# A hybrid decoder layer: the opening in finer slices, and other priorities for the second half

## The chip, the core and the metric

The kernel runs on one core of a Trainium2 chip. Its time is device microseconds of one execution. The engines are TensorE (PE, with weight loads as PEld), VectorE (DVE), ScalarE (ACT), GpSimd (POOL) and SyncE (SP), which here issues nearly all DMAs. A change of about 1% of this kernel's time can be told from none.

## The reference

One layer works on x, 1024 rows (positions) of 1024 columns, all in float32. `mod` below is a product of a conditioning vector with w_ada (1024 x 6144), cut into six rows of 1024: shift, scale and gate of the two sub-layers.

```
h    = rmsnorm(x, g_mix) * (1 + sc1) + sh1
proj = h @ w_in                      # q 512, k 128, v 128, qi 512, ki 64, wi 8, cu 1024 columns
q, k, qi, ki = rope on the first quarter of each 64-wide head
score[t, s] = sum over 8 heads of wi[t] * relu(qi[t] . ki[s] / 8),  only s <= t
sel  = the 256 best s of each t      # causal top-k
attn = softmax(q . k[sel] / 8) @ v[sel]              # 8 heads, 2 key heads
conv = silu(layernorm(depthwise causal conv, width 31, of glu(cu)))   # 512 channels
x    = x + gt1 * (concat(attn, conv) @ w_out)
h    = rmsnorm(x, g_mlp) * (1 + sc2) + sh2
x    = x + gt2 * (square(relu(h @ w_up)) @ w_down)                    # width 4096
out  = rmsnorm(x, g_final)
```

## The kernel before

The 1024 rows are 8 blocks of 128, in two halves: blocks 0 to 3 and 4 to 7. Columns of 1024 are 8 pieces k of 128. Nearly every product is made of three: both operands are split into a rounded high part and the low part that is left, and high x high, high x low and low x high are summed in PSUM. So for every weight piece ScalarE writes the high part and GpSimd the low part (`load_unit`, L161 to L186; `load_w`, L147).

The code is written in the Tile framework, which orders each engine's instructions by itself: each instruction has a priority number (`tc.cur_priority`, from the table `PR` in L54; a lower number goes first among those that a model of the chip holds ready), and instructions of one engine then run in that fixed order. Buffers are handed out in the order of the code: a tile with `bufs=2` waits for the tile two before it, whatever the priorities. The weight units share one ring: two raw buffers and three of high and low parts, each cut into halves (L163 to L175).

**The opening** (`start` pool, L239 to L420) makes h, transposed and split (`hT`), and the products with the 328 columns of w_in for k, v, ki and wi.
- `START` (L49) is the order of SyncE's loads: x0 to x7 are the blocks of x, a0 to a3 the slices of w_ada for shift and scale (each four loads of 512 KB into two of the four `wa` buffers), p0 to p2 the three pieces of k/v weights.
- `row_scale` (L283) takes four blocks' mean squares (even blocks by ScalarE, L290, odd ones by VectorE, L287), their inverse roots, and a diagonal matrix `dg` for each block (L296). `transposes` (L305) multiplies x by `dg`, which transposes and scales it at once, and ScalarE copies the result to `xT`.
- `ada` (L312) is VectorE's running sum over the eight pieces of a slice of w_ada, in SBUF; `ada_end` (L321) has TensorE add up the 128 partitions and puts shift and scale for two pieces k into `modT`.
- `h_cols` (L331) scales and shifts one piece k of one half on VectorE (L334), takes the high part on ScalarE (L335) and the low part (L336) on VectorE for the first half's pieces below `LOV` = 6, on GpSimd for the others.
- `kv` (L340) makes the products of four blocks with one piece k.
- `WORK` (L50) is the order of these steps. Behind them stand the second half's `h_cols`, the angles and their sine and cosine (L373 to L412).

**After the opening** come the second half's k/v products (priority `k`), the keys for attention and indexer, and three more parts of w_ada, 24 loads of 512 KB with VectorE's sums behind them (`ada_part`, L512; the load is L517, the sum L521, TensorE's part of it L537). The rest follows `ORDER` (L46) and `TAIL` (L44): Q and q are the projections of indexer queries and queries (0 for the first half, 1 for the second; they go out to DRAM, L563, and come back by block, L567), g the gate units of the convolution, c the convolution of the first half (31 taps on VectorE, L643), i the index scores of a block, s a search of the 256th best score of two blocks by 31 halvings (ScalarE counts, L680; VectorE steps, L682 and L683), S the selection from it (L686 to L711), a the attention of a block, n and z the convolution's norm and output, o the output projection, h the norm ahead of the MLP. The first half's MLP (11 of its 16 groups of columns, `f11`) has nearly the lowest priority and fills TensorE while the second half's search, selection and attention run. What is left of the MLP runs at the end, from about 904 us.

Of the kernel before, what the change touches and what calls it, by code (L numbers as in the profile page):

```python
# [9 lines left out]
FT = mybir.dt.float32  # L10
# [3 lines left out]
U8 = mybir.dt.uint8  # L14
AF = mybir.ActivationFunctionType
# [37 lines left out]
LOV = 6  # L53
PR = {'feed': 32050, 'evac': 30050, 'k': 150500, 'qi': 33500, 'ada': 130000, 'idx': 200000, 'idx2': 207550, 'small': 149500, 'sign': 150050, 'sign0': 205450, 'select': 401450, 'select0': 207500, 'att0': 205500, 'norm0': 190500, 'out0': 207000, 'res0': 30000, 'conv0': 998450, 'conv1': 401000, 'q': 400000, 'qi1': 401000, 'q1': 401500, 'glu': 206500, 'glu1': 410000, 'att1': 33450, 'norm1': 998500, 'out1': 150000, 'res1': 206000, 'upx': 215900, 'vhl': 411500, 'hd0': 213500, 'hd7': 399950, 'sq3': 997950, 'mlp': 1000000}  # L54
# [18 lines left out]
def layer(ctx, tc, x, c, positions, w_ada, b_ada, g_mix, w_in, conv_w, conv_b,  # L73
# [165 lines left out]
    with tc.tile_pool(name="start", bufs=1, reuse_waits="tile") as st:  # L239
# [37 lines left out]

        xT = st.tile([128, KD, S], FT, name="xT")
        ms, rs, tmp1 = (st.tile([128, 8], FT, name=n) for n in ("ms", "rs", "tmp1"))
        junk = st.tile([128, D], U8, name="junk")  # L280
        dg = {}

        def row_scale(g0):  # L283
            for b in range(g0, g0 + 4):
# [6 lines left out]
            col = slice(g0, g0 + 4)  # L291
            V.tensor_scalar(ms[:, col], ms[:, col], 1.0 / D, EPS, op0=OP.mult, op1=OP.add)
            rsqrt(rs[:, col], ms[:, col], tmp1[:, col], 4)
            for b in range(g0, g0 + 4):
                dg[b] = st.tile([128, 128], FT, name="dg", bufs=4)
                V.tensor_scalar(dg[b], ident, rs[:, b:b + 1], None, op0=OP.mult)  # L296

        for hf in range(2):  # L300
            hT[hf] = (half_tile("AC"[hf]), half_tile("BD"[hf]))
        pa = psum.tile([128, 16], FT, name="po")

        def transposes(b):
            for q in range(2):  # L305
                t = tp_tile()
                for j in range(4):
                    k = 4 * q + j
                    T.matmul(t[:, j, :], xs[b][:, k * 128:(k + 1) * 128], dg[b], start=True, stop=True)  # L309
                A.copy(xT[:, 4 * q:4 * q + 4, b * 128:(b + 1) * 128], t)  # L310

        def ada(jj):  # L312
            acc = st.tile([128, 512], FT, name="acc", bufs=2)
            for k in range(KD):
                if k:
                    V.scalar_tensor_tensor(acc, was[jj, k // 4 * 4][:, k % 4, :], cond[:, k:k + 1], acc, op0=OP.mult, op1=OP.add)  # L316
                else:
                    V.tensor_scalar(acc, was[jj, k // 4 * 4][:, k % 4, :], cond[:, 0:1], None, op0=OP.mult)
            return acc

        def ada_end(jj, acc):  # L321
            for i in range(4):
                c0 = 8 * (i // 2) + 2 * jj + i % 2
                T.matmul(pa[:, c0:c0 + 1], acc[:, i * 128:(i + 1) * 128], ones[:, 0:1], start=True, stop=True)
            s0, s1 = slice(2 * jj, 2 * jj + 2), slice(8 + 2 * jj, 10 + 2 * jj)
            V.tensor_tensor(modT[:, s0], pa[:, s0], bada[:, s0], op=OP.add)
            a1 = modT[:, s1]
            V.tensor_tensor(a1, pa[:, s1], bada[:, s1], op=OP.add)
            V.scalar_tensor_tensor(a1, a1, 1.0, gmix[:, s0], op0=OP.add, op1=OP.mult)

        def h_cols(k, hf):  # L331
            hi, lo = hT[hf]
            xk = xT[:, k, hf * 512:(hf + 1) * 512]
# [4 lines left out]
        kvps = {}  # L338

        def kv(k, blocks):  # L340
            for i, b in enumerate(blocks):
                if k == 0:
                    kvps[b] = (mm_tile if i < 2 else mc_tile)(328)
                hi, lo = hblk(b, k, 0), hblk(b, k, 1)
                wh, wl = pieces[k]
                for j, (l, r) in enumerate(((hi, wh), (lo, wh), (hi, wl))):
                    T.matmul(kvps[b], l, r, start=k == 0 and j == 0, stop=k == KD - 1 and j == 2)

        row_scale(0)
        accs = {}  # L350
        for step in WORK.split():
            n = int(step[1:])
            if step[0] == "a":
                accs[n] = ada(n)
            elif step[0] == "t":
                transposes(n)
            elif step[0] == "r":
                row_scale(n)
            elif step[0] == "e":
                ada_end(n, accs[n])  # L360
            elif step[0] == "h":
                for k in (2 * n, 2 * n + 1):
                    h_cols(k, 0)
            elif step[0] == "k":
                for k in (2 * n, 2 * n + 1):
                    kv(k, KVG[0])
            elif step[0] == "g":
                for k in (2 * n, 2 * n + 1):
                    h_cols(k, 1)
        for k in range(KD):  # L370
            if k // 2 not in [int(x[1:]) for x in WORK.split() if x[0] == "g"]:
                h_cols(k, 1)
# [36 lines left out]
        A.activation(sn, rr, AF.Sin)  # L409
        A.activation(ml, rr, AF.Abs)  # L410
        V.tensor_scalar(ml, ml, -1.0, 1.5707963267948966, op0=OP.mult, op1=OP.add)
        A.activation(cs, ml, AF.Sin)  # L412
# [852 lines left out]
```

## Time and profile before

| | us |
|---|---|
| median of 3 runs | 1372.71 (1371.03 to 1380.61) |
| profiled execution | 1377.54 |
| its span | 1375.8 |
| TensorE busy (matmuls) | 1268.3, 92% |
| VectorE busy | 974.8, 71% |
| ScalarE busy | 683.5, 50% |
| GpSimd busy | 482.0, 35% |
| DMA | 139.55 MB, mean 101 GB/s |
| mean granted TensorE clock | 0.964 |

Times in a trace are microseconds from the start of the span, durations of single instructions nanoseconds where marked. An engine's busy share is an average over stages with different limits; what counts is which wait ends last in a stage. A matmul counts as busy from its start to a modelled end, and matmuls overlap, so their number in a stretch says more than their busy time. The granted clock is the share of TensorE's full speed that it was allowed; its two levels are 1.2 and 2.4 GHz.

### The profile page before, as it was taken

The numbers are of one execution on the slowest core, as the hardware profiler recorded it, in microseconds if no ns is written. First come the engines' busy times: TensorE is split into PE (matmuls) and PEld (weight loads), VectorE is DVE, ScalarE is ACT, GpSimd is POOL, SyncE is SP. The second block draws the span as 40 slices with busy tenths as digits, with TensorE's granted clock in tenths as the row PEclk, the third lists the DMA queues.
The fourth block names the chain that finished last, engine by engine and source line by source line (L and its number), as shares of the span: only waits on it lengthen the run. The fifth ranks groups of instructions, "written<-read, shape, count | busy, mean of one in ns | idle before, by whom it ended". The sixth has DMA issues, their size and how long they took to land.

```text
span 1375.8 us, 19421 instructions
## 1 busy us (share of the span) xinstructions
PE 1268.3 (92%) x6686; PEld 1065.7 (77%) x6686; DVE 974.8 (71%) x2074; ACT 683.5 (50%) x1376; POOL 482.0 (35%) x396
## 2 busy tenths in 40 slices
PE   4677899989998899989999999899999999999997
PEld 4676789978887678767887879777878877888875
DVE  4879889999898899997878762473443386343457
ACT  3323358855764888768983552333122223333332
POOL 1333434422144234452223216422222244444453
PEclk9688999999999899999999999999999999999999
DMA  9337735522143123222111122352111134323332
GB/s 319 121 115 224 226 79 155 139 62 70 31 139 110 60 70 93 92 70 61 62 47 54 62 77 85 130 192 83 47 45 49 54 107 162 93 91 101 94 98 91
DMA packets 135690, 139.55 MB, mean 101 GB/s; under 512 B 8877, under 2 KB 109833, under 8 KB 135592
## 3 DMA queue, kind: packets, MB, share of 16 engines
q1 hardware_dynamic: 135424, 138.22, 32.2%
q8 instruction: 52, 0.85, 0.3%
q14 instruction: 46, 0.38, 0.1%
q10 hardware_dynamic: 168, 0.11, 0.0%
HBM read 126.23 MB, written 12.06 MB: 101 GB/s over the span
## 4 chain that ended last, share of the span: by engine, by line
PE 68%; DVE 21%; DMA 4%; issue 3%; ACT 3%; POOL 1%; ACTq 0%; POOLq 0%; DVEq 0%; SPq 0%
PE mm L126 25%; PE mc L126 13%; PE mm L137 9%; PE tp L126 7%; DMA wa<-in_w_ada_dram 3%; PE po L841 2%; PE tp L834 2%; DVE acc L521 2%; DVE cv L643 1%; PE tp L309 1%; PE po L748 1%; PE mc L592 1%; DVE acc L1018 1%; PE mc L822 1%; DVE acc L316 1%
## 5 line engine op out<-in xcount | busy, mean ns | idle before, releaser
L185 POOL TENSOR_TENSOR wlo<-wraw,whi 128x512 fp32r<-128x512 f32 x310 | 416.7, 1352 | 754.2 <-ACT whi L184 698.0
L184 ACT ACTIVATE whi<-wraw 128x512 fp32r<-128x512 f32 x310 | 193.9, 629 | 292.1 <-PE mm L126 143.1
L126 PE MATMUL mm<-half,whi 128*128 128x512 f32 x608 | 207.4, 407 | 0.6 <-ACT half L957 0.6
L680 ACT ACTIVATE sj<-score,bits 128x512 uint8<-128x512 f32 (+5 forms) x186 | 163.2, 877 | 23.0 <-DVE bits L683 11.0
L643 DVE SCALAR_TENSOR_TENSOR cv<-glu,cwT,cv 128x512 f32<-128x512 f32 x232 | 174.0, 750 | 0.8
L126 PE MATMUL mm<-whi,uh 128*128 128x512 f32 x344 | 141.7, 412 | 14.3 <-DVE sq L979 8.2
L126 PE MATMUL mc<-half,whi 128*128 128x512 f32 x416 | 149.0, 390 | 0.1
L126 PE MATMUL mm<-whi,ul 128*128 128x512 f32 x344 | 138.8, 404 | 3.0 <-DVE ul L986 3.0
L126 PE MATMUL mm<-wlo,uh 128*128 128x512 f32 x344 | 139.4, 405 | 0.0
L984 DVE TENSOR_TENSOR sq<-sq 128x512 f32<-128x512 f32 x42 | 46.0, 1096 | 126.1 <-ACT sq L983 126.1
L1018 DVE TENSOR_TENSOR acc<-mm,acc 128x512 f32<-128x512 f32 x152 | 104.3, 687 | 39.8 <-PE mm L126 38.9
L126 PE MATMUL mc<-half,wlo 128*128 128x512 f32 x336 | 131.1, 390 | 0.0
L126 PEld LDWEIGHTS mm<-half,whi 128*128 128x128 f32 x608 | 114.2, 192 | 20.0 <-ACT half L957 0.8
L137 PE MATMUL mm<-whi,half 128*128 128x256 f32 x640 | 121.8, 286 | 3.2 <-DVE wi L450 3.0
L126 PE MATMUL mm<-half,wlo 128*128 128x512 f32 x304 | 123.1, 405 | 0.0
L137 PEld LDWEIGHTS mm<-whi,half 128*128 128x128 f32 x640 | 102.9, 194 | 5.7 <-issue 3.1
L126 PE MATMUL mc<-h,whi 128*128 128x512 f32 x256 | 99.9, 390 | 0.0
L126 PEld LDWEIGHTS mm<-whi,uh 128*128 128x128 f32 x344 | 66.5, 193 | 37.0 <-DVE sq L979 10.8
L137 PE MATMUL mm<-wlo,half 128*128 128x256 f32 x320 | 91.2, 285 | 0.0
L126 PEld LDWEIGHTS mc<-half,whi 128*128 128x128 f32 x416 | 78.0, 188 | 16.6 <-ACT half L957 0.5
L126 PEld LDWEIGHTS mm<-whi,ul 128*128 128x128 f32 x344 | 66.6, 194 | 18.7 <-DVE ul L986 4.3
L126 PEld LDWEIGHTS mm<-wlo,uh 128*128 128x128 f32 x344 | 66.8, 194 | 13.2
(312 smaller groups left out, 2657.4 us busy)
## 6 DMA issues: line engine op xcount, KB each, us to landing
wraw<-in_w_up_dram SPq DMA_DIRECT2D x108, 256.0 KB, 2.8
wraw<-in_w_down_dram SPq DMA_DIRECT2D x108, 256.0 KB, 2.8
wa<-in_w_ada_dram SPq DMA_DIRECT2D x48, 512.0 KB, 4.5
wraw<-in_w_in_dram SPq DMA_DIRECT2D x33, 256.0 KB, 2.8
wraw<-in_w_in_dram SPq DMA_DIRECT2D x64, 128.0 KB, 2.9
wraw<-in_w_out_dram SPq DMA_DIRECT2D x32, 256.0 KB, 2.7
xs<-in_x_dram SPq DMA_DIRECT2D x8, 512.0 KB, 4.5
x<-in_x_dram SPq DMA_DIRECT2D x8, 512.0 KB, 4.3
```

Of the source, the lines that this page charges most:

```text
L126: T.matmul(ps, x, y, start=first and i == 0, stop=last and i == 3 * n - 1)
L137: T.matmul(ps[:, i * 256:(i + 1) * 256], rows[i][k][x], w[k][y], start=m == 0, stop=m == len(steps) - 1)
L184: A.activation(hi, raw, AF.Copy)
L185: P.tensor_tensor(lo, raw, hi.bitcast(FT), op=OP.subtract)
L309: T.matmul(t[:, j, :], xs[b][:, k * 128:(k + 1) * 128], dg[b], start=True, stop=True)
L521: V.scalar_tensor_tensor(accs[s], w, cond[:, k:k + 1], accs[s], op0=OP.mult, op1=OP.add)
L643: V.scalar_tensor_tensor(y if tap == CK - 1 else s, gl[:, tap:tap + 512], cwT[:, j, tap:tap + 1], s, op0=OP.mult, op1=OP.add)
L680: A.activation(sj[:, :L], score[b], AF.Sign, bias=bits[:, col].bitcast(FT), accum_out=cnt[:, col])
L834: T.transpose(t[:, 2 * i + u, :], sbp[u][:, (i0 + i) * 128:(i0 + i + 1) * 128], ident)
L841: T.matmul(po[:, hp % 2], vhl[:, i0 + i, g].rearrange("p a d -> p (a d)"), p[:, 2 * i:2 * i + 2, :], start=i0 + i + j == 0, stop=i0 + i == ...
L984: V.tensor_tensor(sq, sq, sq, op=OP.mult)
L1018: V.tensor_tensor(acc[b][:, cols], ps, acc[b][:, cols], op=OP.add)
```

## The change

In the opening:
- ScalarE takes all squares, and scales x itself by the inverse root (`row_scale`), so that the transposes are plain ones; `dg` is gone.
- The angles are computed ahead of everything else; only sine and cosine are left as a step of their own (T).
- `ada` is cut into three steps (pieces 0 and 1, 2 to 4, 5 to 7), and its running sum lies in PSUM.
- `h_cols` becomes `h_hi` and `h_lo`. ScalarE makes the high part straight from the transposed x, VectorE makes the whole value and the low part, for all pieces and both halves. The second half's x is transposed piece by piece and read from PSUM, so `xT` holds one half.
- `START` loads p0 right after x0, a1 ahead of four blocks of x, and p1 ahead of the rest of x.

In the order of the rest: q1 stands ahead of S3 in `ORDER`. In `PR`, the selection of blocks 4 to 7 goes from 401450 to 52550, the second half's convolution norm from 998500 to 129950, the first half's q projection from 400000 to 412000, the first half's search from 205450 to 207050, its gate units from 206500 to 205500, the second half's output projection from 150000 to 206450, and the MLP from 1000000 to 998000.

```diff
-ORDER = "Q0 g0 i2 c q0 i3 s3 Q1 m S3 q1 a0 g1 a1 n0 a2 z0 a3 i6 i7 o i5 h i4 s7 s5"
+ORDER = "Q0 g0 i2 c q0 i3 s3 Q1 m q1 S3 a0 g1 a1 n0 a2 z0 a3 i6 i7 o i5 h i4 s7 s5"
-START = "x0 x1 x2 x3 a0 p0 x4 x5 x6 x7 a1 p1 a2 p2 a3"
-WORK = "a0 t0 t1 t2 t3 e0 h0 a1 e1 k0 h1 a2 e2 k1 r4 t4 t5 h2 a3 e3 k2 h3 k3 t6 t7"
+START = "x0 p0 x1 x3 x2 a0 a1 x4 x6 x5 p1 a2 p2 x7 a3"
+WORK = "a0a a0b a0c t0 t1 t2 t3 T a1a e0 x0 a1b l0 k0 a1c s4 a2a e1 x1 a2b l1 k1 a2c a3a e2 x2 a3b l2 k2 p4 a3c e3 x3 l3 k3 X0 L0 X1 L1 X2 L2 X3 L3"
...
-                if b % 2:
-                    xv = xs[b].rearrange("p (u n) -> p u n", u=2)
-                    V.tensor_tensor_reduce(xT[:, b - b % 2:b - b % 2 + 2, 512:], xv, xv, 1.0, 0.0, op0=OP.mult, op1=OP.add,
-                                           accum_out=ms[:, b:b + 1])
-                else:
-                    A.activation(junk, xs[b], AF.Square, accum_out=ms[:, b:b + 1])
+        def squares(g0):
+            for b in range(g0, g0 + 4):
+                A.activation(junk, xs[b], AF.Square, accum_out=ms[:, b:b + 1])
+            col = slice(g0, g0 + 4)
+            V.tensor_scalar(ms[:, col], ms[:, col], 1.0 / D, EPS, op0=OP.mult, op1=OP.add)
+            P.tensor_tensor(rs[:, col], ms[:, col], half_c[:, :4], op=OP.pow)
...
+            for b in range(g0, g0 + 4):
+                A.activation(xs[b], xs[b], AF.Copy, scale=rs[:, b:b + 1])
...
-                    T.matmul(t[:, j, :], xs[b][:, k * 128:(k + 1) * 128], dg[b], start=True, stop=True)
+                    T.transpose(t[:, j, :], xs[b][:, k * 128:(k + 1) * 128], ident)
...
+        def ada(jj, ks):
+            if 0 in ks:
+                accs[jj] = (st.tile([128, 512], FT, name="acc", bufs=2), cv_tile())
+            acc, ps = accs[jj]
+            for k in ks:
+                w = was[jj, k // 4 * 4][:, k % 4, :]
+                if k:
+                    V.scalar_tensor_tensor(acc if k == KD - 1 else ps, w, cond[:, k:k + 1], ps, op0=OP.mult, op1=OP.add)
+                else:
+                    V.tensor_scalar(ps, w, cond[:, 0:1], None, op0=OP.mult)
...
-            V.tensor_scalar(xk, xk, modT[:, 8 + k:9 + k], modT[:, k:k + 1], op0=OP.mult, op1=OP.add)
-            A.activation(hi[:, k, :], xk, AF.Copy)
-            (V if hf == 0 and k < LOV else P).tensor_tensor(lo[:, k, :], xk, hi[:, k, :].bitcast(FT), op=OP.subtract)
+        def h_hi(k, hf):
+            if hf == 0:
+                xk = xT[:, k, :]
+            else:
+                t = tp_tile()
+                for b in range(4):
+                    T.transpose(t[:, b, :], xs[4 + b][:, k * 128:(k + 1) * 128], ident)
+                xk = t.rearrange("p a b -> p (a b)")
+            A.activation(hT[hf][0][:, k, :], xk, AF.Identity, bias=modT[:, k:k + 1], scale=modT[:, 8 + k:9 + k])
+            xks[k, hf] = st.tile([128, 512], FT, name="xk", bufs=4)
+            V.tensor_scalar(xks[k, hf], xk, modT[:, 8 + k:9 + k], modT[:, k:k + 1], op0=OP.mult, op1=OP.add)
+
+        def h_lo(k, hf):
+            hi, lo = hT[hf]
+            V.tensor_tensor(lo[:, k, :], xks[k, hf], hi[:, k, :].bitcast(FT), op=OP.subtract)
```

In the new `WORK`, a digit and a letter name a slice and its part (a0a), t and x are the first half's transposes and `h_hi`, l its `h_lo`, X and L the second half's, s4 and p4 the squares and the scaling of blocks 4 to 7.

## Rows read from the trace of the kernel before

**Rows 1.** The page: busy time and share of each engine.
```profile
PE 1268.3 (92%) x6686; PEld 1065.7 (77%) x6686; DVE 974.8 (71%) x2074; ACT 683.5 (50%) x1376; POOL 482.0 (35%) x396
```

**Rows 2.** Windows by stage; busy us (instructions) by engine, granted clock, DMA share.
```profile
core 0: us, PE busy (x) PEld busy (x) DVE busy (x) ACT busy (x) POOL busy (x), PEclk, DMA share, GB/s
0.00:29.40 29.40, 11.54 (x73) 11.24 (x73) 11.87 (x28) 11.52 (x18) 4.67 (x12) 1.00 0.94 316
29.40:56.00 26.60, 21.37 (x121) 20.23 (x122) 22.53 (x41) 11.90 (x20) 8.13 (x6) 0.70 0.63 199
56.00:86.40 30.40, 16.28 (x69) 14.88 (x68) 26.53 (x60) 5.12 (x10) 11.65 (x8) 0.70 0.16 50
...
200.00:575.00 375.00, 356.75 (x2184) 310.55 (x2184) 346.96 (x830) 274.62 (x598) 135.46 (x116) 0.97 0.31 93
...
904.00:1330.00 426.00, 422.96 (x1825) 343.36 (x1825) 200.86 (x262) 124.43 (x211) 154.27 (x118) 1.00 0.30 94
```

**Rows 3.** The chain that ended last: start, length, what the time went to.
```profile
92.55 4.38 DMA wa<-in_w_ada_dram
...
175.28 1.50 PE po L537 x8
...
948.12 21.79 PE mc L126 x96
```

**Rows 4.** Waits of SyncE's queue, 55 to 175 us: total, times, longest.
```profile
SPq L517 <- POOL half L336: 22.3, 1, 22.3
```

**Rows 5.** Timeline of GpSimd: start, length, instruction, idle before it.
```profile
77.17 5.21 POOL L336 TENSOR_TENSOR half<-xT,half 128x512 fp32r<-128x512 f32 x4 [4.00 <-ACT half L335]
```

**Rows 6.** Groups by line and shape, 0 to 130 us: busy, mean ns, idle before.
```profile
L336 POOL TENSOR_TENSOR half<-xT,half 128x512 fp32r<-128x512 f32 x10 | 14.5, 1474 | 19.1 <-ACT half L335 19.1
...
L287 DVE CUSTOM_DVE_ANT_0 xT<-xs 128x1024 f32<-128x1024 f32 x4 | 4.9, 1223 | 8.4 <-DMA xs<-in_x_dram 8.4
...
L144 POOL TENSOR_TENSOR wlo<-wraw,whi 128x984 fp32r<-128x984 f32 x2 | 4.5, 2260 | 20.5 <-DMA wa<-in_w_ada_dram 11.3 <-ACT whi L143 9.2
...
L290 ACT ACTIVATE junk<-xs 128x1024 uint8<-128x1024 f32 x4 | 4.2, 1058 | 1.3 <-DMA xs<-in_x_dram 1.3
```

**Rows 7.** Timeline of VectorE in the opening.
```profile
37.42 5.47 DVE L316 SCALAR_TENSOR_TENSOR acc<-wa,cond,acc 128x512 f32<-128x512 f32 x7
...
65.04 1.00 DVE L334 TENSOR_SCALAR xT<-xT,modT 128x512 f32<-128x512 f32 x2
...
66.62 1.28 DVE L336 TENSOR_TENSOR half<-xT,half 128x512 fp32r<-128x512 f32 x2
...
78.68 1.27 DVE L393 TENSOR_SCALAR mh<-mh 128x64 f32<-128x64 f32 x1
...
83.28 0.19 DVE L385 TENSOR_SCALAR m<-rr 128x64 f32<-128x64 f32 x1
...
85.55 0.20 DVE L408 TENSOR_SCALAR rr<-rr 128x64 f32<-128x64 f32 x1
```

**Rows 8.** Groups of VectorE by line and shape, 430 to 480 us.
```profile
L958 DVE TENSOR_SCALAR tp<-tp,modT 128x512 f32<-128x512 f32 x8 | 6.4, 817 | 2.6 <-ACT half L957 2.6
```

**Rows 9.** The page's costliest groups: the convolution's taps.
```profile
L643 DVE SCALAR_TENSOR_TENSOR cv<-glu,cwT,cv 128x512 f32<-128x512 f32 x232 | 174.0, 750 | 0.8
```

**Rows 10.** Timeline of TensorE: the first indexer query product.
```profile
107.67 0.36 PE L137 MATMUL mm<-whi,half 128*128 128x256 f32 x1 [2.99 <-DVE wi L450]
```

**Rows 11.** Timeline of VectorE: block 7's selection ends, its first attention scores.
```profile
597.85 0.56 DVE L710 TENSOR_SCALAR score<-e 128x1024 bf16<-128x1024 bf16 x1
...
636.22 0.69 DVE L824 CUSTOM_DVE_ANT_0 sb<-mc,score 128x512 f32<-128x512 f32 x1 [0.85 <-PE mc L823]
```

**Rows 12.** Windows around the second half's selections.
```profile
575.00:636.00 61.00, 52.44 (x228) 40.29 (x227) 53.58 (x134) 42.26 (x84) 27.86 (x18) 0.97 0.25 78
...
727.00:746.00 19.00, 16.05 (x62) 12.53 (x61) 16.80 (x33) 4.12 (x8) 6.23 (x5) 0.82 0.14 42
```

**Rows 13.** Timelines: last q stores of blocks 0 to 3; their first scores.
```profile
224.74 0.89 SPq L563 DMA_DIRECT2D q_d<-qe  x2
...
287.18 0.29 DVE L736 CUSTOM_DVE_ANT_0 sb<-mc,caus 128x128 f32<-128x128 f32 x1 [0.47 <-PE mc L735]
```

More of the change, by code (lines that the diff above doesn't have):

```diff
@@ L321, in ada_end @@
[L321 to L329, printed above, removed]
@@ L349, in layer @@
[L349 to L369, printed above, removed]
@@ new lines, in layer, with transposes @@
+        for hf in range(2):
+            hT[hf] = (half_tile("AC"[hf]), half_tile("BD"[hf]))
+        pa = psum.tile([128, 16], FT, name="po")
+        def transposes(b):
+            for q in range(2):
+                t = tp_tile()
+                for j in range(4):
+                    k = 4 * q + j
+                    T.transpose(t[:, j, :], xs[b][:, k * 128:(k + 1) * 128], ident)
+                A.copy(xT[:, 4 * q:4 * q + 4, b * 128:(b + 1) * 128], t)
+        accs = {}
+        def ada(jj, ks):
[8 more added lines that the diff above has]
+                    V.tensor_scalar(ps, w, cond[:, 0:1], None, op0=OP.mult)
@@ new lines, in ada_end @@
+        def ada_end(jj):
+            acc = accs[jj][0]
+            for i in range(4):
+                c0 = 8 * (i // 2) + 2 * jj + i % 2
+                T.matmul(pa[:, c0:c0 + 1], acc[:, i * 128:(i + 1) * 128], ones[:, 0:1], start=True, stop=True)
+            s0, s1 = slice(2 * jj, 2 * jj + 2), slice(8 + 2 * jj, 10 + 2 * jj)
+            V.tensor_tensor(modT[:, s0], pa[:, s0], bada[:, s0], op=OP.add)
+            a1 = modT[:, s1]
+            V.tensor_tensor(a1, pa[:, s1], bada[:, s1], op=OP.add)
+            V.scalar_tensor_tensor(a1, a1, 1.0, gmix[:, s0], op0=OP.add, op1=OP.mult)
@@ new lines, in h_lo, with kv @@
+        def h_lo(k, hf):
+            hi, lo = hT[hf]
+            V.tensor_tensor(lo[:, k, :], xks[k, hf], hi[:, k, :].bitcast(FT), op=OP.subtract)
+        kvps = {}
+        def kv(k, blocks):
+            for i, b in enumerate(blocks):
+                if k == 0:
+                    kvps[b] = (mm_tile if i < 2 else mc_tile)(328)
+                hi, lo = hblk(b, k, 0), hblk(b, k, 1)
+                wh, wl = pieces[k]
+                for j, (l, r) in enumerate(((hi, wh), (lo, wh), (hi, wl))):
+                    T.matmul(kvps[b], l, r, start=k == 0 and j == 0, stop=k == KD - 1 and j == 2)
@@ new lines, in opening @@
+        def opening():
+            squares(0)
+            row_scale(0)
+            for step in WORK.split():
+                if step == "T":
+                    trig()
+                    continue
+                n = int(step[1])
+                if step[0] == "a":
+                    ada(n, {"a": (0, 1), "b": (2, 3, 4), "c": (5, 6, 7)}[step[2]])
+                elif step[0] == "t":
+                    transposes(n)
+                elif step[0] == "s":
+                    squares(n)
+                elif step[0] == "p":
+                    row_scale(n)
+                elif step[0] == "e":
+                    ada_end(n)
+                elif step[0] in "xX":
+                    for k in (2 * n, 2 * n + 1):
+                        h_hi(k, step[0] == "X")
+                elif step[0] in "lL":
+                    for k in (2 * n, 2 * n + 1):
+                        h_lo(k, step[0] == "L")
+                elif step[0] == "k":
+                    for k in (2 * n, 2 * n + 1):
+                        kv(k, KVG[0])
@@ L414, in layer @@
+        with ExitStack() as es:
+            if MANUAL:
+                es.enter_context(tc.manual_schedule(engines={getattr(mybir.EngineType, e) for e in MANUAL}))
+            opening()
         tw = tp_tile()
```

70 lines of the change are left out of this document (18 added, 52 removed).

## The prediction

> **What bounds the kernel now.** I read the page first, then the windows, the chain of waits, SyncE's own waits, and last the timeline of the first 90 us. The page gives TensorE as busy for 92% of the span [rows 1], but a busy matmul there is not a matmul at its peak, so the unit I count in is the chain's run of 96 three-term products in 21.79 us, 0.227 us for 512 columns [rows 3]. By it the last long stage, 904 to 1330, holds 1825 matmuls, 414 us of work in 426: TensorE sets that stage, and it can only be moved, not shortened. From 200 to 575 VectorE is busy for 347 of 375 us; it sets that stretch, and the change takes next to nothing off VectorE there. What is left is the start. Up to 86.4 us TensorE's 263 matmuls are short, the granted clock is 0.70 from 29.4 on (a mix of 1.2 and 2.4 GHz), and VectorE is busy for 22.5 of 26.6 and 26.5 of 30.4 us [rows 2]. So VectorE is the bound of the opening, and the memory is not: 199 and 50 GB/s after 316 at first.
>
> How does the opening hand its delay on? The chain runs through the next stage's loads of w_ada, from 92.55 on, to the small sums that end at 176.8 [rows 3]. These 24 loads cannot start before the opening's memory is free: SyncE stood 22.3 us at the first of them, until GpSimd had done its last low-part subtraction [rows 4], which ended at 77.17 + 5.21 = 82.4 us [rows 5]. That moment is what the change can move; all later stages follow from it with the same work.
>
> **The change part by part.** *VectorE's list in the opening.* It loses four squares of 1.22 us (4.9 us) and eight scaled diagonals [rows 6]; the angles (some thirty ops of 0.2 us) move into the time in which VectorE waits 8.4 us for x [rows 6]. If that cover is gone, they cost the 7.1 us that most of them take now, from 78.68 to 85.75 [rows 7]. It gains ten low-part subtractions from GpSimd. I count the new list from the landing of the first ada slice. That is now used at about 17.3; 504 KB of k/v weights go ahead of it, 1.6 us at 316 GB/s, so 19. Then: 32 multiply-adds at (5.47 - 0.75)/6 = 0.79 us, 25.2; eight scale-and-adds of 0.50, 4.0; eight subtractions of 0.64, 5.1; 17 small ops of 0.19, 3.2 [rows 7]; in the second half eight scale-and-adds that read PSUM, 0.82 each [rows 8], 6.5, and eight subtractions, 5.1. Sum 49, plus 2 for the sums on TensorE that the two early ops of the next slice don't cover: the first half's columns end near 58, the second half's near 70.
>
> The running sum of the ada slices is moved into PSUM; the convolution's taps do the same there at 0.750 us [rows 9], no dearer than the 0.75 in SBUF, so I put that move at nothing. The scale-and-adds on PSUM are dearer: 0.82 against 0.50. The Trainium skill's "VectorE: DVE Perf Modes", section "Why PSUM operands drop a tier", says that a PSUM operand shuts out the double-rate form; at the SBUF price twelve such ops would be 3.8 us cheaper, by its rule they are not, and the trace agrees (817 ns).
>
> *Contention.* While GpSimd subtracts, small VectorE ops take 1.27 us instead of 0.19 [rows 5, 7]. All ten of these GpSimd ops (14.5 us) go [rows 6]. Only the three splits of the k/v weights stay there, 2.26 us at most each: between 0 and 6.8 us for VectorE, and I take 0, as the multiply-adds that fill most of the list ran at 0.79 in the stretch without GpSimd work and nothing shows them slower in PSUM. The Trainium skill's "SBUF — State Buffer", section "Who interferes with whom", speaks against the change here: a VectorE op with two SBUF inputs, as the moved subtractions are, waits for the whole of a GpSimd op that reads SBUF. By that rule the sum would be up to 6.8 us worse.
>
> *ScalarE* gets four more squares and eight scalings of 1.06 us [rows 6], 13 us, where it is busy for 28.5 of the first 86.4 us [rows 2]. On the path are one square and one scaling before the first transposes, 2 us while VectorE is on the first slice; without that cover, 2. The transposes and the high parts keep their count, at no cost.
>
> *Queues.* On SyncE p0 passes x1 to x3 (1.6 us, counted), a1 passes x4 to x7, and x7 goes behind a2, whose buffer waits for slice 0. Behind x7 stand a3 on SyncE and, on ScalarE, the square of x7 with the high parts queued after it. The opening's 13.9 MB (24 loads of 512 KB and 1.3 MB of k/v weights) at 316 GB/s need 44 us; VectorE reaches a3 at about 44. I price this at 0 to 5 and take 0. GpSimd's queue only gets shorter.
>
> *The memory's release.* The next stage's first load waits for whatever tile lies under it: at the earliest the first half's x, free near 57, at the latest the last subtraction, 70. Against 82.4 that is a gain of 12 to 25; I take **20**, since the row shows a wait on x's tile, which now goes early. Nearer the other end, TensorE's first query product, which waits at 107.67 for the second half's k/v banks [rows 10], would come near 78, 30 us sooner; that is the upper bound.
>
> *Middle of the kernel.* Selection and convolution norm of the second half move up. Selection of block 7 ends at 598.4, but its first scores are taken at 636.2 [rows 11]; in between stand the last transposes of the norm, in the same PSUM tiles. In 575 to 636 there are 228 matmuls, at most 52 us of work in 61, and in 727 to 746 62, 14 in 19 [rows 12]: some 14 us idle. VectorE is busy 53.6 of the 61, so the reordering mostly changes who waits. Bounds: 14 won or 14 lost; nearest to the VectorE row I take **4** won.
>
> *Edits at nothing.* The later q projection, its place before the selection, and the priorities of the first half's search, the gate units, the output projection and the MLP. The weights pass through one ring of buffers in the order of the code, and this holds the q units where they are: units ahead of Q1 cannot fall behind it. If that cover is gone, it is the slower rival below.
>
> Sum: the profiled execution took 1377.54 us (1375.8 of span, 1.7 around it). 1377.5 - 20 - 4 = 1353.5. The median of the three runs is 4.8 below that execution, so I forecast 1353.5 - 4.8, about **1348**.
>
> **The rivals.** A, the forecast, 1338 to 1359: chance 0.52.
> B, the release stays late: the new loads lie under the second half's tiles, or the w_ada stream, two buffers deep, is what counts. Gain 12, none later: 1377.5 - 12 - 4.8 = 1361. For it: SyncE's wait was for the very last op. Against: that op was on the slowest engine. 0.20.
> C, both ends come out well, 30 and 14: 1329. 0.12. Against it: VectorE's 93% from 200 on.
> D, slower: the first half's q projection does fall behind Q1, q1 and the second gate units. Their 192 + 192 matmuls of 256 and 192 of 512 columns take 23 + 23 + 44 = 90 us. The last store of q now starts at 224.7, the first scores at 287.2 [rows 13], so 62 us are slack and the scores would come some 40 us late, after other work is used up: 1377.5 - 20 - 4 + 40 - 4.8 = 1389. It decides once the last q store of blocks 0 to 3 passes about 285. 0.06.
> E, the early selection pushes the MLP's own evictions back and loses the 14: 1377.5 - 20 + 14 - 4.8 = 1367. 0.10.
>
> **The numbers.** About 1% (14 us) is what a measurement of this kernel can tell from no change. Faster than 1359: nearly all of A (0.49), C, and 0.4 of B: 0.69. Slower than 1386: D and a little for several losses together, 0.07. The rest, 0.24, is within 1%. The range runs from C's middle to just past E, 1328 to 1368; left out are D, half of C and a tail.
>
> **What would show it.** Right, step by step: no TENSOR_TENSOR of the opening on GpSimd but the weight splits; VectorE's small ops at 0.2 us; the first half's last k/v product near 62, the second's near 74; SyncE's first w_ada load after the opening at 57 to 70; the search of blocks 3 and 2 some 20 us sooner; TensorE's stage from 904 as long as now. Block 7's first scores should follow its selection within 15 us instead of 38. Wrong: w_ada loads that still start near 80, a stretch 86 to 200 that grows by what the opening lost, the last store of q for the first half past 285, or 575 to 900 longer than now.

## The result, and the profile after

| | us |
|---|---|
| before, median of 4 runs | 1371.87 (1370.92 to 1380.61) |
| after, median of 4 runs | 1356.92 (1355.55 to 1358.33) |
| after / before | 0.9878, 95% interval 0.9844 to 0.9912 |
| profiled execution of after | 1357.23, span 1355.5 (before 1377.54, span 1375.8) |
| mean granted TensorE clock | 0.972 (before 0.964) |

The change makes the kernel 15 us faster; forecast were 24.7 us and a time of 1348, inside the range and 9 us too good. On a second chip the same two kernels stood at 1374.25 and 1354.0, ratio 0.985 [0.9818, 0.9883]. The ratios leave out three executions that took far longer than the rest of their kernel: 4241.3 us (low parts on GpSimd, below), 1556.12 us (sum in SBUF, below) and one of before of 6866.07 us.

The busy times of after's page, against [rows 1]: VectorE has 10 us less work, ScalarE 9 more, GpSimd 18 less.
```profile
PE 1251.4 (92%) x6622; PEld 1050.2 (77%) x6622; DVE 964.6 (71%) x2068; ACT 692.6 (51%) x1384; POOL 464.4 (34%) x386
```
The windows of after, columns as in [rows 2] and [rows 12].
```profile
0.00:29.40 29.40, 7.56 (x39) 6.49 (x40) 16.14 (x53) 16.53 (x26) 4.67 (x12) 1.00 0.93 309
29.40:56.00 26.60, 18.56 (x95) 16.89 (x96) 22.82 (x46) 13.86 (x21) 5.15 (x3) 0.81 0.72 227
56.00:86.40 30.40, 22.70 (x136) 20.62 (x136) 23.96 (x53) 11.78 (x22) 3.00 (x2) 0.89 0.33 96
200.00:575.00 375.00, 356.44 (x2148) 307.71 (x2147) 346.86 (x825) 269.49 (x582) 138.35 (x116) 0.98 0.31 93
575.00:636.00 61.00, 54.68 (x265) 42.99 (x263) 50.81 (x126) 40.16 (x75) 19.50 (x15) 0.94 0.22 65
904.00:1330.00 426.00, 417.93 (x1795) 337.68 (x1794) 203.84 (x266) 121.75 (x205) 160.28 (x121) 1.00 0.27 84
```
Work is done sooner: 136 matmuls instead of 69 fall into 56 to 86 us, 265 instead of 228 into 575 to 636. VectorE's 347 us in 200 to 575 are the same, as forecast.

SyncE's waits from 55 to 175 us (total, times, longest), where before had 22.3 us for GpSimd [rows 4]:
```profile
SPq L541 <- DVE xk L391: 14.2, 1, 14.2
SPq L541 <- DVE half L395: 9.0, 1, 9.0
```
SyncE's first loads of the next stage, in before and in after (each row holds two loads; the second of after stands behind the wait of 9.0 us):
```profile
82.41 0.82 SPq L517 DMA_DIRECT2D wa<-in_w_ada_dram  x2
```
```profile
59.85 9.76 SPq L541 DMA_DIRECT2D wa<-in_w_ada_dram  x2
```
GpSimd's timeline up to 80 us, against [rows 5]: the weight splits and two small steps, no low parts.
```profile
11.78 2.26 POOL L144 TENSOR_TENSOR wlo<-wraw,whi 128x984 fp32r<-128x984 f32 x1 [9.83 <-ACT whi L143]
...
39.88 3.85 POOL L144 TENSOR_TENSOR wlo<-wraw,whi 128x984 fp32r<-128x984 f32 x2 [21.53 <-DMA wa<-in_w_ada_dram]
```
VectorE's opening, against [rows 7]: an angle step beside the first weight split, first slice, second to last slice, its wait for TensorE's sums, the last low part, and the first sum of the next stage's w_ada.
```profile
11.89 2.23 DVE L293 SCALAR_TENSOR_TENSOR rr<-ml,rr 128x64 f32<-128x64 f32 x1
...
19.16 0.75 DVE L366 TENSOR_SCALAR cv<-wa,cond 128x512 f32<-128x512 f32 x1
...
40.31 4.71 DVE L364 SCALAR_TENSOR_TENSOR cv<-wa,cond,cv 128x512 f32<-128x512 f32 x6
...
47.77 0.16 DVE L374 TENSOR_TENSOR modT<-po,vT 128x2 f32<-128x2 f32 x1 [1.96 <-PE po L372]
...
71.17 1.28 DVE L395 TENSOR_TENSOR half<-xk,half 128x512 fp32r<-128x512 f32 x2
...
75.33 0.88 DVE L547 TENSOR_SCALAR acc<-wa,cond 128x512 f32<-128x512 f32 x2
```
In the kernel before that first sum stood at 89.66, so the opening hands over 14.3 us sooner:
```profile
89.66 0.88 DVE L523 TENSOR_SCALAR acc<-wa,cond 128x512 f32<-128x512 f32 x2
```
TensorE's first query product, SyncE's last q stores of blocks 0 to 3, and the end of block 7's selection with its first scores, against [rows 10, 13, 11]:
```profile
93.98 0.36 PE L137 MATMUL mm<-whi,half 128*128 128x256 f32 x1 [2.80 <-DVE wi L474]
```
```profile
217.41 0.89 SPq L587 DMA_DIRECT2D q_d<-qe  x2
```
```profile
573.76 1.04 DVE L734 TENSOR_SCALAR score<-e 128x1024 bf16<-128x1024 bf16 x1
...
615.75 0.69 DVE L848 CUSTOM_DVE_ANT_0 sb<-mc,score 128x512 f32<-128x512 f32 x1
```
The selection ends 24 us sooner, the scores come 20 us sooner and still 41 us behind it.

**One account for all kernels.** From 200 us on, TensorE's granted clock falls now and then from 2.4 to 1.2 GHz. Windows of 10 us give at most what that takes away: the sum of (1 - granted clock) x 10 us, "lost" below (where TensorE waits anyway, a low clock costs nothing; the last window reaches past the end of the span, which adds about 1 us to every row). With the start of the first search (the first count on ScalarE) the span splits into start + lost + rest. All from one profiled execution each; the ratios are of all runs. The kernels ran on several chips and after on two of them, so kernels of different chips are compared by their ratio to before on the same chip.

| kernel | ratio to before, 95% interval | span | start | lost | rest |
|---|---|---|---|---|---|
| before | | 1375.8 | 194.2 | 22.2 | 1159.4 |
| after | 0.9878 [0.9844, 0.9912] | 1355.5 | 180.6 | 19.7 | 1155.2 |
| after, again | 0.985 [0.9818, 0.9883] | 1352.2 | 180.8 | 16.4 | 1155.0 |
| opening alone | 0.9941 [0.9919, 0.9963] | 1370.1 | 180.7 | 32.0 | 1157.4 |
| priorities alone | 0.9917 [0.9888, 0.9946] | 1362.9 | 190.7 | 18.4 | 1153.8 |
| opening, selection and norm | 0.9968 [0.9941, 0.9995] | 1377.2 | 184.5 | 30.4 | 1162.3 |
| after, q put back | 0.994 [0.9914, 0.9966] | 1369.1 | 178.6 | 26.0 | 1164.5 |
| before, q alone | 0.995 [0.9927, 0.9974] | 1368.4 | 191.8 | 16.6 | 1160.0 |
| opening and q | 0.9872 [0.9838, 0.9906] | 1358.0 | 182.0 | 15.1 | 1160.9 |
| after without selection and norm | 0.9863 [0.9834, 0.9892] | 1358.8 | 181.0 | 16.1 | 1161.7 |

The 20.3 us between the two profiled spans are 13.6 of start, 2.5 of clock and 4.2 of rest.

A profiled execution need not be a typical one: that of the opening alone is the longest of its eleven, that of opening, selection and norm the longest of its twelve, and that of before lies 5.7 us above its median. The mean clocks of all runs give an estimate free of this: (1 - mean clock) x span, less what the profiled execution lost in its first 200 us (29 in before, 19 in the others). It is 18 us for before and 25 for the opening alone on the same chip, 21 for before and 16 for opening and q on theirs: the same direction as in the table, by smaller amounts.

### The profile page after: what moved, and what is told of

It is laid out like the page before. It is cut to its first block, busy times and chain, and to the rows that moved or that the text cites. A ratio compares the mean times of both kernels' runs of the same rounds, so it can differ in the third digit from the quotient of the medians.

```text
span 1355.5 us, 19285 instructions
## 1 busy us (share of the span) xinstructions
PE 1251.4 (92%) x6622; PEld 1050.2 (77%) x6622; DVE 964.6 (71%) x2068; ACT 692.6 (51%) x1384; POOL 464.4 (34%) x386
## 4 chain that ended last, share of the span: by engine, by line
PE 66%; DVE 20%; DMA 4%; ACT 4%; issue 3%; POOL 1%; ACTq 0%; POOLq 0%; SPq 0%; DVEq 0%
PE mm L126 25%; PE mc L126 14%; PE tp L126 7%; PE mm L137 5%; DMA wa<-in_w_ada_dram 3%; DVE cv L667 2%; PE po L865 2%; PE tp L858 2%; DVE acc L545 1%; ACT sj L704 1%; PE po L772 1%; DVE acc L1042 1%; PE mc L846 1%; PE mc L847 1%; DVE e L682 1%
## 5 line engine op out<-in xcount | busy, mean ns | idle before, releaser
L126 PE MATMUL mm<-half,whi 128*128 128x512 f32 x608 | 204.8, 405 | 0.1
L126 PE MATMUL mc<-half,whi 128*128 128x512 f32 x416 | 150.4, 393 | 0.5 <-ACT half L981 0.5
L126 PE MATMUL mm<-whi,uh 128*128 128x512 f32 x344 | 138.5, 403 | 7.1 <-DVE acc L1042 3.2
L126 PE MATMUL mm<-whi,ul 128*128 128x512 f32 x344 | 137.4, 399 | 3.3 <-DVE ul L1010 3.3
L126 PE MATMUL mm<-wlo,uh 128*128 128x512 f32 x344 | 136.8, 398 | 0.0
L126 PE MATMUL mc<-half,wlo 128*128 128x512 f32 x336 | 132.1, 393 | 0.0
L126 PEld LDWEIGHTS mm<-half,whi 128*128 128x128 f32 x608 | 115.3, 193 | 20.2 <-ACT half L981 0.3
L126 PE MATMUL mm<-half,wlo 128*128 128x512 f32 x304 | 124.4, 409 | 0.0
L126 PE MATMUL mc<-h,whi 128*128 128x512 f32 x256 | 100.2, 391 | 0.0
L126 PEld LDWEIGHTS mc<-half,whi 128*128 128x128 f32 x416 | 79.0, 190 | 17.3 <-ACT half L981 0.8
L137 PE MATMUL mm<-wlo,half 128*128 128x256 f32 x320 | 90.6, 283 | 0.4 <-POOL wlo L185 0.4
L126 PEld LDWEIGHTS mm<-whi,uh 128*128 128x128 f32 x344 | 65.3, 190 | 26.1 <-DVE acc L1042 6.5
L126 PEld LDWEIGHTS mm<-whi,ul 128*128 128x128 f32 x344 | 65.3, 190 | 18.1 <-DVE ul L1010 4.2
L126 PEld LDWEIGHTS mm<-wlo,uh 128*128 128x128 f32 x344 | 65.2, 190 | 13.0
```

The costliest lines, as they stand in the source:

```text
L126: T.matmul(ps, x, y, start=first and i == 0, stop=last and i == 3 * n - 1)
L137: T.matmul(ps[:, i * 256:(i + 1) * 256], rows[i][k][x], w[k][y], start=m == 0, stop=m == len(steps) - 1)
```

## The experiments

**Opening alone.** The new opening with the old `ORDER` and `PR`:
```diff
-ORDER = "... Q1 m q1 S3 a0 ..."    # and the whole new PR
+ORDER = "... Q1 m S3 q1 a0 ..."    # and the whole old PR
```


> The new opening alone, with the old priorities and the old order of the rest. Theory (the opening gives nearly all: VectorE starts the next stage's w_ada sums 14 us sooner and the rest follows): 1358 us, 1354 to 1362, with the first w_ada sum near 75 us, block 7's first scores near 622. Rival (the opening's gain is lost by the old order of the middle, and the early selection and norm bring it): 1366 or more.

Measured 1367.37 against 1374.25, ratio 0.9941: 7 us, though its search starts 13.5 us sooner, and block 7's first scores come at 629.5 where 622 was expected. The time is the rival's, but its reason falls two runs below: early selection and norm don't bring the rest back. The table has where it went: TensorE loses 32.0 us of clock instead of 22.2 (25 instead of 18 by the estimate from all runs).

**Priorities alone.** The kernel before with the new `ORDER` and `PR`:
```diff
-ORDER = "... Q1 m S3 q1 a0 ..."    # and the old PR
+ORDER = "... Q1 m q1 S3 a0 ..."    # and the new PR
```


> The old opening with all the new priorities and the new order, nothing else. Theory (opening gives nearly all): 1370 us, 1365 to 1374; the first w_ada sum stays near 90 us, block 7's first scores come some 6 us sooner than in the kernel before. Rival (selection and norm early bring most): 1362 or less.

Measured 1363.84, ratio 0.9917: 10 us, where the forecast had 4 for all of them. It lies between the two expected ranges.

**Opening, early selection and norm, nothing else.** The changed kernel with the old `ORDER` and five of the seven numbers put back:
```diff
-'sign0': 207050, 'q': 412000, 'glu': 205500, 'out1': 206450, 'mlp': 998000
+'sign0': 205450, 'q': 400000, 'glu': 206500, 'out1': 150000, 'mlp': 1000000
```


> The changed kernel with only the selection and the second half's norm early; the other five priorities and the place of the second q projection as in the kernel before. Theory (those edits cost nothing, the ring of weight buffers holds the order): as the changed kernel, 1357 us, within 4. Rival (they matter): off by more than 4 us either way.

Measured 1370.81, ratio 0.9968: the rival. So the six edits that the forecast costed at nothing (these five and the place of q1) are worth 16 us beside the rest of the change.

**The changed kernel again**, on the chip of these three:

> The changed kernel itself, once more, on the chip of the other runs. Theory: 1357 us, 1.1% below the kernel before, first w_ada sum near 75 us. Rival (the 15 us are a matter of the chip they were measured on): a ratio above 0.994.

Measured 1354.0, ratio 0.985: the gain is not a matter of the chip.

**Which of the six?** Put back singly, `ORDER`, `glu`, `sign0` and `mlp` leave the instructions of all five engines in exactly the order of the changed kernel: these four do nothing by themselves, and they were not run. `out1` changes a short stretch. `q` reorders everything behind the first half's queries, so it went to the chip.

**After, q put back**:
```diff
-'q': 412000
+'q': 400000
```


> The changed kernel with one number put back: the first half's q projection at 400000 instead of 412000. Theory 1 (this number alone is what the edits counted at nothing were worth): about 14 us are lost, ratio to the kernel before 0.996, near the run with five edits undone (0.997), and TensorE loses some 9 us more than the changed kernel between 430 and 505. Rival (the output projection's priority carries it, or a sum of small ones): at most 5 us lost, ratio 0.986 to 0.990.

Measured 1368.14 against 1376.08, ratio 0.994: of the change's gain 8 to 12 us are gone, somewhat less than theory 1 had. Both its lost clock (26.0) and its rest (1164.5) are larger; between 430 and 505 TensorE loses 5 us more, not 9. What is left to the 16 us would be `out1`, the only other of the six that changes an order; the intervals of the two runs overlap, and it was not run alone.

**Before, q alone**:
```diff
-'q': 400000
+'q': 412000
```


> The kernel before with this one number changed: q from 400000 to 412000, nothing else. Theory 1 (q works alone): most of what all new priorities give on the old opening (ratio 0.992), so 0.990 to 0.994. Theory 2 (q is worth something only with the early selection and the early norm of the second half): no change, 0.998 to 1.002.

Measured 1369.77, ratio 0.995: theory 1, somewhat weaker than expected; theory 2 falls, since q works without the early selection and norm.

**Opening and q**: the kernel "opening alone" with the same one number.

> The new opening with q at 412000 and every other priority and the order as before. Theory 1: opening (7 to 8 us) and q (10 or more) add up, ratio 0.985 to 0.988, as the whole change. Theory 2: as the opening alone, 0.994.

Measured 1359.53, ratio 0.9872. The two add up (0.9941 x 0.995 = 0.989), and nothing else is needed for what the whole change gives, as far as these intervals tell. The stretch in which they differ most is 425 to 500 us. One window of before, of before with q alone, of the opening alone, and of opening and q (the last three figures of a row: granted clock, DMA share, GB/s):
```profile
425.00:500.00 75.00, 63.61 (x319) 51.07 (x319) 66.36 (x156) 57.01 (x116) 23.92 (x23) 0.86 0.25 83
```
```profile
425.00:500.00 75.00, 66.93 (x334) 52.88 (x333) 68.42 (x168) 62.42 (x125) 26.23 (x24) 0.93 0.27 88
```
```profile
425.00:500.00 75.00, 64.97 (x290) 51.30 (x289) 66.89 (x161) 59.10 (x117) 23.65 (x22) 0.84 0.25 81
```
```profile
425.00:500.00 75.00, 68.38 (x316) 53.36 (x315) 70.26 (x172) 64.45 (x125) 29.25 (x25) 0.93 0.27 87
```
With q late TensorE does 15 and 26 matmuls more in these 75 us, at 0.93 of full clock instead of 0.86 and 0.84. The waits of TensorE from 464 to 480, where the first MLP group passes from its up products to its down products, for the opening alone and then for after on the same chip (total, times, longest):
```profile
PE mm L126 <- DVE ul L1010: 1.4, 1, 1.4
PE mm L126 <- ACT uh L1004: 1.3, 1, 1.3
PE mc L616 <- DVE flag L706: 0.8, 1, 0.8
```
```profile
PE mm L126 <- DVE ul L1010: 0.8, 1, 0.8
PE mm L126 <- ACT acc L1040: 0.6, 2, 0.3
```
3.5 us of waiting against 1.4. In the first the granted clock is 0.76 from 470 to 480, in the second it stays at 1.00 from 464 to 480.

**After without early selection and norm**:
```diff
-'select': 52550, 'norm1': 129950
+'select': 401450, 'norm1': 998500
```


> The changed kernel with the second half's selection and convolution norm late again (401450 and 998500). My forecast gave them 4 us: ratio 0.989 to 0.991. Theory 1 (they are worth nothing beside q): 0.985 to 0.988, with block 7's first scores again some 35 us after its selection. Theory 2 (they and q need each other): 0.994.

Measured 1359.6, ratio 0.9863, theory 1: within the intervals of the changed kernel, so these two are worth nothing that can be told apart in the time, though its profiled execution has a rest 6 us larger. Block 7's selection ends at 580.7, its first scores come at 621.4, again 41 us later.

**Filling the stall.** The changed kernel with extra products in the first half's norm ahead of the MLP:
```diff
+    warm = lambda n: [T.matmul(d, key, keys, start=True, stop=True) for d in [tp_tile()...] for _ in range(n)]
-            t = tp_tile()
+            t = tp_tile() if hf or k > 5 or not warm(4) else tp_tile()
```


> The changed kernel with 24 extra products of 512 columns, four ahead of the transposes of each of the first six pieces of the first half's MLP norm; nobody reads them. They fill TensorE where it stands between 428 and 443 us, with its granted clock at 0.69 and 0.80 of full speed in 430 to 450 (5 us of full speed lost there). Theory 1 (part of the gain in the middle is TensorE's clock, which falls after such a stall): the granted clock stays above 0.9 there, and the later groups come 2 to 4 us sooner, ratio 0.981 to 0.985. Rival (the stall itself is what costs, and it belongs to VectorE and ScalarE): the extra 24 x 0.227 = 5.4 us of products add up to 5 us, ratio 0.985 to 0.990.

Measured 1372.07 against 1374.16, ratio 0.9978: 14 to 18 us worse than the changed kernel, more than either theory had. It did not do what it was for:
```profile
425.00:500.00 75.00, 65.04 (x283) 50.53 (x282) 69.29 (x169) 64.14 (x125) 24.09 (x21) 0.86 0.23 71
```
The granted clock is 0.86 here, 0.66 in 430 to 450, lower than without the extra work (0.74), and "lost" is 23.8 in all. The planner reordered VectorE and ScalarE around the 24 products, and 30 matmuls fewer, the 24 included, fit into the stretch than in after (313). The run says nothing on theory 1; it says that an edit that brings a new order can cost as much as the whole change wins.

**Every second whole value of the second half on ScalarE.**
```diff
-            V.tensor_scalar(xks[k, hf], xk, modT[:, 8 + k:9 + k], modT[:, k:k + 1], op0=OP.mult, op1=OP.add)
+            A.activation(xks[k, hf], xk, AF.Identity, bias=..., scale=...) if hf and k % 2 else V.tensor_scalar(...)
```


> The changed kernel with every second whole value of the second half's h made on ScalarE instead of VectorE. Theory 1 (VectorE's list, not the release of memory, now sets the end of the opening): four times 0.72 us less, the first sum of the next stage at 72 to 73.5 instead of 75.3, the first search 2 to 3 us sooner. Rival (the loads or ScalarE set it): the first sum stays at 75 or comes later.

Measured 1348.39 against 1374.16, ratio 0.9826 [0.979, 0.9862]. The first sum of the next stage is not sooner (75.67), since VectorE now waits for ScalarE, as the rival had it:
```profile
65.74 0.81 DVE L391 TENSOR_SCALAR xk<-tp,modT 128x512 f32<-128x512 f32 x1 [1.82 <-ACT half L389]
...
75.67 0.88 DVE L547 TENSOR_SCALAR acc<-wa,cond 128x512 f32<-128x512 f32 x2
```
And yet the profiled execution is 5.8 us shorter than that of after on the other chip, 5.5 of them ahead of the first search. Apart from the four moved values and one weight load of the next stage (with its high and its low part), which changes places with a neighbour, all engines run the same order, so this is the closest look at the clock in the study. At 153 us TensorE waits for VectorE's score sums. After (second profile), TensorE's timeline and two windows:
```profile
156.34 0.44 PE L616 MATMUL mc<-keys,qT 128*128 128x384 f32 x1 [2.37 <-DVE score L623]
```
```profile
153.00:156.00 3.00, 0.97 (x5) 0.46 (x3) 3.00 (x4) 1.55 (x3) 2.05 (x3) 1.00 0.82 259
156.00:168.00 12.00, 11.66 (x39) 9.95 (x40) 6.89 (x13) 3.44 (x6) 3.90 (x4) 0.57 0.36 92
```
The same of the kernel with values on ScalarE:
```profile
155.09 0.44 PE L616 MATMUL mc<-keys,qT 128*128 128x384 f32 x1 [1.37 <-DVE score L623]
```
```profile
153.00:156.00 3.00, 1.63 (x8) 1.09 (x7) 3.00 (x4) 0.78 (x2) 2.79 (x3) 1.00 0.90 264
156.00:168.00 12.00, 11.69 (x59) 9.46 (x58) 10.46 (x18) 6.10 (x11) 4.11 (x4) 1.00 0.39 102
```
And the first profile of after:
```profile
156.10 0.44 PE L616 MATMUL mc<-keys,qT 128*128 128x384 f32 x1 [1.82 <-DVE score L623]
```
```profile
156.00:168.00 12.00, 11.90 (x40) 10.07 (x41) 6.72 (x13) 3.53 (x6) 4.03 (x5) 0.57 0.35 91
```
After a wait of 2.37 us TensorE goes on at 0.57 of full clock for 12 us and gets 39 matmuls done, after one of 1.82 us the same with 40; after one of 1.37 us it stays at 2.4 GHz and does 59. Half a microsecond more of waiting goes with five more of time. In which executions the shorter wait occurs can't be chosen: this kernel's own four runs took 1348.24, 1348.53, 1346.83 and, at a lower mean clock (0.971 against 0.976), 1357.6.

**Low parts of the second half on GpSimd again**, all else as in the changed kernel:
```diff
-            V.tensor_tensor(lo[:, k, :], xks[k, hf], hi[:, k, :].bitcast(FT), op=OP.subtract)
+            (P if hf else V).tensor_tensor(lo[:, k, :], xks[k, hf], hi[:, k, :].bitcast(FT), op=OP.subtract)
```


> The changed kernel with the second half's eight low-part subtractions of the opening on GpSimd again, as in the kernel before. Theory 1 (VectorE's own list sets the opening, and GpSimd is the slower place): the subtractions end near 76 instead of 72, VectorE's first sum of the next stage comes at 74 to 79, total within 4 us of the changed kernel. Rival (VectorE's list alone counts, what GpSimd does is hidden): 5 us of subtractions go off VectorE and the first sum comes near 71. If the two engines hinder each other, VectorE's scale-and-adds of 0.8 us get longer.

Measured 1347.73 against 1374.16, ratio 0.9806 [0.9775, 0.9837]: the shortest time of the study. By the ratios it is 6 to 10 us shorter than the changed kernel; its interval overlaps that of after's second measurement, not that of the first. So this part of the change undone is at least no worse, and theory 1's 4 us are passed. The one trace is of the execution of 4241.3 us (the others took 1347.5 to 1347.95): TensorE's products of 512 columns take about 1.1 us there where after's take 0.4, so its times can't be compared, and where the gain comes from stays open. For VectorE's scale-and-adds it still shows that GpSimd does not hinder them: one beside a subtraction of GpSimd takes 0.81 us, as long as that of the last run (65.74, above) without one.
```profile
107.36 0.81 DVE L391 TENSOR_SCALAR xk<-tp,modT 128x512 f32<-128x512 f32 x1 [0.87 <-ACT half L389]
```
```profile
106.56 1.27 POOL L395 TENSOR_TENSOR half<-xk,half 128x512 fp32r<-128x512 f32 x1 [11.51 <-DVE xk L391]
```

**The sum of the slices in SBUF again**:
```diff
-                accs[jj] = (st.tile([128, 512], FT, name="acc", bufs=2), cv_tile())
+                accs[jj] = (st.tile([128, 512], FT, name="acc", bufs=2),) * 2
```


> The changed kernel with the running sum of the opening's w_ada slices in SBUF again. Theory 1 (the move to PSUM costs and brings nothing, as the forecast had it): multiply-adds of 0.79 us as with PSUM, also beside GpSimd's weight splits, first sum of the next stage at 75 to 77, total within 4 us. Rival (with both inputs in SBUF a multiply-add stands still while GpSimd splits weights): the multiply-adds beside the splits of 3.85 us take twice as long or more, and the first sum comes 2 to 6 us later.

Measured 1359.49, ratio 0.9893 [0.9853, 0.9932]. The first sum of the next stage comes at 83.26 instead of 75.33, 8 us later. VectorE's timeline, one slice beside GpSimd's weight splits, one without and the first sum, and then those splits:
```profile
42.61 8.60 DVE L364 SCALAR_TENSOR_TENSOR acc<-wa,cond,acc 128x512 f32<-128x512 f32 x7
...
57.55 5.48 DVE L364 SCALAR_TENSOR_TENSOR acc<-wa,cond,acc 128x512 f32<-128x512 f32 x7
...
83.26 0.87 DVE L547 TENSOR_SCALAR acc<-wa,cond 128x512 f32<-128x512 f32 x2
```
```profile
42.45 4.28 POOL L144 TENSOR_TENSOR wlo<-wraw,whi 128x984 fp32r<-128x984 f32 x2 [24.47 <-ACT whi L143]
```
Seven multiply-adds take 8.60 us beside 4.28 us of splits and 5.48 without: 3.1 us. With the sum in PSUM, six of them at 40.31 beside 3.85 us of splits take 4.71, 0.785 each, as long as the six at 19.94 with no split beside them. The Trainium skill's "SBUF — State Buffer", section "Who interferes with whom", has both halves of this: a VectorE op with two SBUF inputs contends with a GpSimd op that reads SBUF, one with a single SBUF input, outside the two-port modes, does not. The runs agree, with 3.1 us for the first and none for the second. So the rival has the mechanism, and more than its 2 to 6 us for the first sum. The other 5 us are mostly longer waits for TensorE (8.7 against 6.2 in the opening) and ScalarE in an opening that is also ordered otherwise. By the end 2 to 6 of the 8 us are left, by the ratios.

## Why the prediction was right, and which steps were not

**Right.** VectorE's list: from 19.16 (forecast 19) to the first half's columns at 60.5 (58) and the second half's at 72.4 (70). Errors cancel in it: it waits 7.4 us (6.2 for TensorE's sums, 1.2 for ScalarE) where 2 were allowed, and its work is some 3 us shorter than 49. The 19 is luck: the first multiply-add waits for no load, VectorE comes to it straight from the inverse roots, for which it had waited 2.95 us for ScalarE and 1.01 for GpSimd. The angles fit ahead of it. GpSimd's ten low parts are gone. Contention: 0 was taken, and 0 was paid, but for other reasons than the one given. The moved subtractions never run beside a weight split (11.78 to 14.04 and 39.88 to 43.73), so neither the 0 nor the 6.8 us was tried on them. A moved angle step did: 2.23 us at 11.89 instead of 0.22, in time in which VectorE then waits for ScalarE anyway. And the multiply-adds pay nothing since their sum lies in PSUM; in SBUF they lose 3.1 us. The first half's last k/v product starts at 62.8 (near 62). The q stores keep their sequence (q, indexer queries, q) and the last of the first half starts at 217.41, so rival D, which wanted it past 285, does not happen. Nor is there a sign of E: 575 to 636 holds 37 matmuls more, not fewer. TensorE's last stage is only moved: at full clock before and after.

**"The memory's release": mis-sized.** Taken 20, measured 14.3 at the first sum, 13.6 at the first search. The first load of the next stage does start 22.6 us sooner (59.85 against 82.4), as x's tile is free early, but this is not what the next stage waits for: the second load waits 9.0 us for a low part, and VectorE takes up the sum only after its list (72.4) and 3 us of k/v evictions. These loads land 3.8 to 5.2 us after they are issued, so the first was there by 65. The last engine to be free set the hand-over, not the first tile. This is read from the timelines; no run with a shorter list on VectorE has a trace in which the sum comes sooner. The price was nearer to rival B's 12, and B's mechanism is there in part, as the second load does wait for a low part of the second half. In the same place, "the second half's last k/v product near 74" was wrong: these 96 products begin at 73.6, once VectorE has emptied the first half's banks (2.55 us of waiting), and end at 90.6. That also rules out the upper bound of 30.

**"Edits at nothing": wrong.** The cover named there, the ring of buffers that holds the q units in place, does hold. But the step took "same sequence of units" for "same time". The q priority only lets the last two stores of the first half slip (217.4 instead of 211.4 with the opening alone), and all engines behind are ordered anew. It is worth about 7 us on the old opening and 9 on the new one. In the table these are mainly clock: lost falls from 22.2 to 16.6 and from 32.0 to 15.1. Four of the other five edits are indeed nothing: they change no order; `out1` was not run alone. That the new order waits less at 470 us is shown; at 270 it waits a little longer (4.42 against 3.87 us, below) and mostly keeps the clock. Why it does so is not settled, and nothing here shows that a later q is better as such.

**"Middle of the kernel": 4 taken, not found.** In the profiled executions the rest falls by 4.2 with the whole change, and rises by 6 when selection and norm are put back; in the medians nothing is left of it. The reason given, that the last transposes of the norm keep block 7's scores waiting, fails: the 15 us asked for were 41, with the early priorities or without.

**What was missing: the clock as a price.** The forecast has no term for it. The opening's 14 us reach the first search in full and then shrink to 7, and the clock lost behind that point is larger by about as much (9.8 in the table, 7 by the estimate from all runs). Half of the 9.8 lies at 270 to 290, where before loses 1.7 us and the opening alone 6.8; the stalls from 425 to 500 cost before nearly as much (0.86 against 0.84). That the clock takes the gain is argued from these sums: no run changed the clock alone. TensorE around attention 0's first scores, the matmul behind the stall and two windows, opening alone, then after:
```profile
271.64 1.23 PE L524 MATMUL tp<-identr,qs 128*128 128x128 f32 x8 [3.87 <-DVE qs L519]
```
```profile
266.00:272.00 6.00, 2.13 (x11) 1.52 (x10) 5.97 (x11) 1.15 (x2) 2.42 (x2) 0.86 0.18 44
272.00:284.00 12.00, 12.00 (x52) 10.96 (x52) 9.81 (x33) 7.29 (x25) 0.64 (x1) 0.50 0.17 45
```
```profile
272.70 0.89 PE L524 MATMUL tp<-identr,qs 128*128 128x128 f32 x8 [4.42 <-DVE qs L519]
```
```profile
266.00:272.00 6.00, 2.28 (x11) 1.54 (x9) 5.97 (x14) 1.22 (x3) 0.00 (x0) 1.00 0.17 44
272.00:284.00 12.00, 11.18 (x64) 9.81 (x65) 11.16 (x34) 8.42 (x28) 2.56 (x2) 0.86 0.25 67
```
The instruction and what it waits for are the same, with 11 matmuls in 6 us; behind 3.87 us the one runs at 1.2 GHz for 12 us, behind 4.42 us the other hardly. So the length of a stall alone does not say what the clock does, and what does is open here.

The forecast came out right in part by luck. Of its 24 us, 20 were for the opening, which gives 7 in the end (6 were too much for the release, 7 go again with the clock), and 4 for the middle, which the medians don't show; 7 to 9 for q were not counted. 24 - 13 - 4 + 8 is the 15 measured, and the 1357 are nearer to rival B's 1361 than to the 1348.

## What to carry to other kernels

Follow a hand-over to the engine that is free last: when a load can start sooner, ask what its consumer is doing then. An edit of a priority is known to be free only if it leaves the order of every engine as it was, which a comparison of the two orders shows before any run. If it moves instructions, its price is open until measured: in this kernel of 1370 us nothing that could be told for the early selection and norm, 7 to 9 us won by q, 14 to 18 lost by the 24 extra products. And in a kernel whose TensorE runs near its limit, look at the granted clock behind each stall as well as at its length.

## What the hardware showed that was not expected

- Stalls of 1.82 and 2.37 us were followed by 12 us at a granted clock of 0.57, one of 1.37 us at the same instruction by none: 40 and 39 matmuls against 59. At 268 us it was the other way round: 3.87 us were followed by 0.50, 4.42 us by 0.86.
- The spread of one kernel's runs goes with this clock: 56 different pairs of mean granted clock (0.956 to 0.972) and span (1366.4 to 1382.3 us) of the kernel before have a correlation of -0.90, and a line through them falls by 9.6 us for each 0.01.
- A multiply-add of 128 x 512 costs 0.785 us with its running sum in PSUM even beside GpSimd's splits; with the sum in SBUF seven of them lose 3.1 us to 4.28 us of splits.
- The granted clock does not tell all of TensorE's pace: in the one trace of the kernel with low parts on GpSimd, products of 128 x 512 (L126) take 1104 ns at a recorded clock of 1.00, in after 405 ns. What slowed them is open.
